# One layer with a product-key expert stage on one core: the first expert rows of the second product, and how the experts in use are found

## The chip, the cores and the metric

One core of a Trainium2 chip runs the whole layer in one launch. Its engines are TensorE (PE: matmuls, with PEld for the weight loads), VectorE (DVE), ScalarE (ACT), GpSimd (POOL) and SyncE (SP); they run side by side and wait for each other by semaphores. The metric is the device time of one launch in microseconds, the median of several runs.

## The reference, cut to what matters

A layer of a diffusion backbone on 256 tokens of 2048 features: a token mixer (projection, two recurrent scans, a spatial gate, output projection), and then the expert stage, at whose middle the change stands. Each token picks 16 of 16384 experts in each of 8 heads by a product of two key tables; each expert has one row u and one row v.

```
idx = e1 * PEER_NKEYS + e2
g = jax.nn.softmax(sc, axis=-1)
u_sel = jnp.take(u_tab, idx, axis=0)
act = jax.nn.gelu(jnp.einsum('td,thkd->thk', hb, u_sel))
v_sel = jnp.take(v_tab, idx, axis=0)
return jnp.einsum('thk,thkd->td', (g * act.astype(jnp.float32)).astype(hb.dtype), v_sel)
```

The result is added to the stream, and a final RMSNorm gives the output.

## The kernel before

The expert stage is computed densely on the one side and by lists on the other. fp32 operands are split in a high and a low part (`split`, lines 255 on ScalarE and 256 on VectorE, half a tile at a time), and a product is the sum of three matmuls of parts (`mm3`, lines 284 to 286).

**The u product.** All 16384 u rows are multiplied with all tokens, in 128 tiles of 128 experts (`u_step`, lines 1188 and 1190). A step's result is evacuated by ScalarE (line 1203), its halves are added on GpSimd (line 1204; on VectorE for the first 8 tiles, lines 1200 and 1201), and in the next step Gelu is applied (`u_out`, line 1209) and the tile is stored to the table `agd` in DRAM (line 1210, ScalarE's queue), which holds for every expert the activations and the gates of all tokens.

**Work beneath it.** `fill` hands out other work between the tiles by credits: 3000 a step, against a cost written beside each piece. In this order: the routing (top 16, softmax), then `gates`, `places`, `make_list`, and the first gathers of v rows. `gates` goes over 32 blocks of 8 tokens: VectorE makes one-hot rows of the two key numbers (line 1025, two a block) and scales one by the gates (line 1034), TensorE multiplies them (`products`): line 1057 gives the gates of all experts, and line 1054 counts, for each half of the tokens (16 blocks), how often an expert was picked. ScalarE keeps the gates (`keep`, line 1067, `GC`), in columns of 4 tokens. From the counts `places` gives every expert in use a place in one of three lists: used by the first token tile only (`N_A` = 26 tiles of 128 rows), by both (up to tile 67), by the second only (up to `N_L` = 92 tiles). `SEQ` is the order in which the tiles of the lists are taken. Experts that find no place are counted in `flag`.

**The seam.** After the last u tile, `act_rows` gathers the activation and gate rows of the first two list tiles from `agd` on GpSimd (line 898, the same line as the v gathers), then every engine loads the flag (line 1290) and branches over a fallback (line 1291) that is run only if an expert found no place. Behind the branch the rows of tiles 2 and 3 are gathered.

**The v product.** `weights` multiplies activations and gates of a list tile (line 1220, VectorE), `weights_high` and `weights_low` split the result (lines 1229 on ScalarE, 1234 on VectorE), and `v_tile` multiplies it with the gathered v rows: 12 matmuls of lines 284 to 286 for a tile of one token tile, 24 for a tile of both. `split_next` prepares the tile after next and gathers rows four tiles ahead.

## Time and profile before

| | us |
|---|---|
| median of 3 runs | 1791.05 |
| lowest, highest | 1789.89, 1794.6 |
| the profiled execution | 1794.17 |
| its span | 1792.4 |
| PE, DVE, ACT, POOL busy in it | 1707.9, 1340.4, 922.0, 401.5 |

The profiled execution is 3.1 us above the median, and its span leaves 1.8 us of its time around it. TensorE is busy in 95% of the span. In the slices of the page it is at nine tenths or more nearly everywhere; the drop at the slices from 1384 us on is the seam. The granted TensorE clock is 0.982 in the mean over the span.

### The profile page before, as it was taken

The numbers are of one execution on the slowest core, as the hardware profiler recorded it, in microseconds if no ns is written. First come the engines' busy times: TensorE is split into PE (matmuls) and PEld (weight loads), VectorE is DVE, ScalarE is ACT, GpSimd is POOL, SyncE is SP. The second block draws the span as 40 slices with busy tenths as digits, with TensorE's granted clock in tenths as the row PEclk, the third lists the DMA queues.
The fourth block names the chain that finished last, engine by engine and source line by source line (L and its number), as shares of the span: only waits on it lengthen the run. The fifth ranks groups of instructions, "written<-read, shape, count | busy, mean of one in ns | idle before, by whom it ended". The sixth has DMA issues, their size and how long they took to land.

```text
span 1792.4 us, 26487 instructions
## 1 busy us (share of the span) xinstructions
PE 1707.9 (95%) x10313; PEld 1422.4 (79%) x10313; DVE 1340.4 (75%) x1812; ACT 922.0 (51%) x1232; POOL 401.5 (22%) x341
## 2 busy tenths in 40 slices
PE   4999999999999999999999999999998799999995
PEld 0778566788799888888888888888887688888884
DVE  1347697687788999898888886988443577777776
ACT  5223666643543455555555555444454465656554
POOL 0000000000100002222222221212112565656652
PEclk8999999999999999999999999999999899999997
DMA  9877778888797656655787888865675789888881
GB/s 394 335 307 281 297 274 323 329 322 299 291 338 283 242 202 215 209 187 184 220 236 227 226 242 235 260 216 189 213 276 189 247 307 350 309 304 307 305 315 59
DMA packets 166266, 472.43 MB, mean 264 GB/s; under 512 B 76692, under 2 KB 109640, under 8 KB 115960
## 3 DMA queue, kind: packets, MB, share of 16 engines
q1 hardware_dynamic: 92544, 316.17, 50.3%
q0 software_dynamic: 21120, 128.68, 20.3%
q10 hardware_dynamic: 52472, 25.84, 5.0%
q8 instruction: 82, 1.34, 0.3%
q14 instruction: 48, 0.39, 0.1%
HBM read 432.81 MB, written 37.83 MB: 263 GB/s over the span
## 4 chain that ended last, share of the span: by engine, by line
PE 80%; DVE 11%; DMA 5%; issue 2%; ACT 2%; POOL 0%; SPq 0%; DVEq 0%; POOLq 0%; ACTq 0%
PE bank L1188 23%; PE bank L284 13%; PE bank L286 12%; PE bank L285 12%; PE bank L1190 12%; DVE ra L256 4%; DMA fa<-in_wm_a_dram 2%; DMA fa<-in_wm_c_dram 2%; PE bank L1057 2%; PE bank L364 1%; PE bank L309 1%; DVE fa L290 1%; DVE fa L942 1%; PE bank L527 1%; DVE fa L940 1%
## 5 line engine op out<-in xcount | busy, mean ns | idle before, releaser
L256 DVE TENSOR_TENSOR ra<-fa,ra 128x1024 fp32r<-128x1024 f32 x564 | 702.0, 1259 | 291.9 <-ACT ra L255 286.2
L255 ACT ACTIVATE ra<-fa 128x1024 fp32r<-128x1024 f32 x564 | 591.3, 1057 | 473.7 <-PE bank L1188 187.3
L1188 PE MATMUL bank<-ra 128*128 128x512 f32 x2048 | 731.9, 401 | 0.0
L1190 PE MATMUL bank<-ra 128*128 128x256 f32 x2048 | 576.9, 282 | 5.1 <-DVE ra L256 5.0
L284 PE MATMUL bank<-ra 128*128 128x512 f32 (+1 forms) x1364 | 475.0, 348 | 17.9 <-ACT ra L1229 16.8
L286 PE MATMUL bank<-ra 128*128 128x512 f32 (+1 forms) x1364 | 468.2, 343 | 5.4 <-DVE ra L1234 4.5
L285 PE MATMUL bank<-ra 128*128 128x512 f32 (+1 forms) x1364 | 467.8, 343 | 1.4 <-DVE ra L256 1.4
L1188 PEld LDWEIGHTS bank<-ra 128*128 128x128 f32 x2048 | 385.8, 188 | 92.6 <-ACT ra L255 0.2
L1190 PEld LDWEIGHTS bank<-ra 128*128 128x128 f32 x2048 | 387.7, 189 | 8.5 <-DVE ra L256 8.4
L284 PEld LDWEIGHTS bank<-ra 128*128 128x128 f32 x1364 | 261.8, 192 | 76.7 <-issue 25.8
L1204 POOL TENSOR_TENSOR fa<-fa 128x256 f32<-128x256 f32 x120 | 150.9, 1258 | 724.2 <-ACT fa L1203 724.1
L286 PEld LDWEIGHTS bank<-ra 128*128 128x128 f32 x1364 | 261.5, 192 | 36.7 <-DVE ra L1234 6.5
L285 PEld LDWEIGHTS bank<-ra 128*128 128x128 f32 x1364 | 261.8, 192 | 32.1 <-DVE ra L256 3.1
L1203 ACT ACTIVATE fa<-bank 128x512 f32<-128x512 f32 x120 | 71.8, 598 | 145.8 <-PE bank L1190 139.8
L898 POOL DMA_INDIRECT fa<-agd,fa x92 | 128.3, 1395 | 39.1 <-issue 26.5
L898 POOL DMA_INDIRECT fa<-in_peer_v_dram,fa x92 | 97.4, 1058 | 119.8 <-DVE ra L256 80.1
L1025 DVE TENSOR_TENSOR fa<-fa 128x1024 f16<-128x1024 bf16 x96 | 113.5, 1223 | 0.0
L1034 DVE TENSOR_TENSOR fa<-fa 128x2048 f16<-128x2048 f16 (+1 forms) x48 | 109.2, 2275 | 0.8
L290 DVE SCALAR_TENSOR_TENSOR fa<-fa 128x2048 f32<-128x2048 f32 x32 | 72.9, 2284 | 0.0
L1209 ACT ACTIVATE fa<-fa 128x256 f32<-128x256 f32 x128 | 52.0, 407 | 33.7 <-DVE fa L1201 25.6
L364 PE MATMUL bank<-fa 128*2 128x512 f32 x256 | 39.6, 711 | 25.5 <-DMA fa<-in_wm_a_dram 17.4
L1229 ACT ACTIVATE ra<-fa 128x128 fp32r<-128x128 f32 x92 | 32.4, 352 | 50.9 <-DVE fa L1220 50.7
(264 smaller groups left out, 1168.1 us busy)
## 6 DMA issues: line engine op xcount, KB each, us to landing
fa<-in_peer_u_dram SPq DMA_DIRECT2D x128, 1024.0 KB, 5.1
fa<-in_wm_a_dram SPq DMA_DIRECT2D x32, 1024.0 KB, 7.8
fa<-in_wm_c_dram SPq DMA_DIRECT2D x32, 1024.0 KB, 6.8
fa<-in_wm_d_dram SPq DMA_DIRECT2D x32, 1024.0 KB, 6.8
fa<-in_w_in_dram SPq DMA_DIRECT2D x24, 1024.0 KB, 4.9
fa<-in_w_out_dram SPq DMA_DIRECT2D x16, 1024.0 KB, 6.7
fa<-in_wq_dram SPq DMA_DIRECT2D x16, 1024.0 KB, 7.4
agd<-fa ACTq DMA_DIRECT2D x128, 128.0 KB, 2.4
```

The lines of the kernel that those rows point to most:

```text
L255: S.activation(h, x, AF.Copy)
L256: V.tensor_tensor(l, x, h.bitcast(F32), op=ALU.subtract)
L284: TE.matmul(dst, wh, mh, start=first, stop=False, skip_group_check=skip)
L285: TE.matmul(dst, wh, ml, start=False, stop=False, skip_group_check=skip)
L286: TE.matmul(dst, wl, mh, start=False, stop=last, skip_group_check=skip)
L290: V.scalar_tensor_tensor(junk, w, 1.0, s, op0=ALU.mult, op1=ALU.mult, accum_out=dst)
L898: G.indirect_dma_start(out=dst, out_offset=None, in_=src, in_offset=bass.IndirectOffsetOnAxis(ap=idx, axis=0), bounds_check=bound, oob_is_ ...
L1025: V.tensor_tensor(dst, iota_b[:, 0:n].unsqueeze(1).to_broadcast([P, TB, n]), numbers.unsqueeze(2).to_broadcast([P, TB, n]), op=ALU.is_equal)
L1034: V.tensor_tensor(og, oj.unsqueeze(2).to_broadcast([P, TB, 2, n]), factors.unsqueeze(3).to_broadcast([P, TB, 2, n]), op=ALU.mult)
L1188: TE.matmul(bank, h[:, es], H2[:, k, :, :].rearrange("p z t -> p (z t)"), start=k == 0, stop=False, skip_group_check=True)
L1190: TE.matmul(bank[:, 0:T], l[:, es], HH[:, k, :], start=False, stop=k == KD - 1, skip_group_check=True)
L1204: G.tensor_tensor(st, HALVES[:, 0:T], HALVES[:, T:2 * T], op=ALU.add)
```

## The change

It has two parts.

Experts in use: the count matmuls of `products` are gone. In `keep`, GpSimd adds up the gates that ScalarE has just stored, over the blocks of a half, in `SUMS` (128 experts by 4 token columns, 512 elements), in two additions a block; at the end of a half VectorE reduces the 4 columns to one (`USED`). `places` takes an expert as in use where this sum is over zero.

Seam: experts of the last three u tiles (from `CUT` = 125) that only the first token tile uses are moved to the list of both, so that the first list needs rows of `agd` from the first 125 tiles alone, and the gather's source is cut to those. `SEQ` begins with four tiles of the first list instead of three. Their rows are gathered in the step of tile 125, and the weights of the first two list tiles are made in the last step (`first_weights`, with a buffer of its own, `WP1`). Tiles 125 to 127 are added on VectorE instead of GpSimd and stored from SyncE's queue. The gathers and weights that stood after the loop and after the branch are gone; the two late v gathers go to `split_next`.

```diff
+CUT = NU - 3
 N_L = N_A + N_1
 ONE_0, BOTH, ONE_1 = list(range(N_A)), list(range(N_A, N_0)), list(range(N_0, N_L))
-SEQ = ONE_0[:3]
+SEQ = ONE_0[:4]
 for _i, _b in enumerate(BOTH):
-    SEQ += [_b] + (ONE_0[3:] + ONE_1)[_i:_i + 1]
+    SEQ += [_b] + (ONE_0[4:] + ONE_1)[_i:_i + 1]
 SEQ += [_s for _s in ONE_1 if _s not in SEQ]
...
     PT = [q_(11520, 128)] + [q_(12288 + 128 * i, 128) for i in range(4)]
+    SUMS = q_(12288, 512).rearrange("p (j t) -> p j t", t=4)
+    USED = [q_(11648 + 128 * i, 128) for i in range(2)]
     STAGE = [q_(12032, 256), q_(14976, 256), dg2]
...
     WP = [dg2, eg[:, 0:256]]
-    HALVES = q_(13824, 512)
+    HALVES, WP1 = q_(13824, 512), q_(11264, 256)
     pidx = small(1)
...
             else:
-                by_index(AGR[n % 4][:, 0:T], ag_half, LIST2[:, j:j + 1], 2 * NE + 1)
+                m = CUT * P + 1 if j < N_A else NE + 1
+                by_index(AGR[n % 4][:, 0:T], ag_half[0:2 * m, :], LIST2[:, j:j + 1], 2 * m - 1)
...
         def products(b):
-            counts = pb[4 + b // NB][:, 0:P]
             oj, og = pair(b, P)
...
                 oa = OHA[b % 2][:, i, :]
-                TE.matmul(counts, oa, oj[:, i, :], start=b % NB == 0 and i == 0,
-                          stop=b % NB == NB - 1 and i == TB - 1, skip_group_check=True)
                 for q in range(2):
...
+            quarter = [GC[c % 2][:, :, o * TB + 4 * x:o * TB + 4 * x + 4] for x in range(2)]
+            if b % NB == 0:
+                G.tensor_tensor(SUMS, quarter[0], quarter[1], op=ALU.add)
+            else:
+                for x in range(2):
+                    G.tensor_tensor(SUMS, SUMS, quarter[x], op=ALU.add)
+            if b % NB == NB - 1:
+                V.tensor_reduce(USED[b // NB], SUMS, axis=AX.X, op=ALU.add)
             if o == HT // TB - 1:
...
         one, tot, inc, pos = PT[0], PT[1], PT[2], PT[3]
-        V.tensor_scalar(u0, pb[4][:, 0:P], 0.5, None, op0=ALU.is_gt)
-        V.tensor_scalar(u1, pb[5][:, 0:P], 0.5, None, op0=ALU.is_gt)
+        V.tensor_scalar(u0, USED[0], 0.0, None, op0=ALU.is_gt)
+        V.tensor_scalar(u1, USED[1], 0.0, None, op0=ALU.is_gt)
         V.tensor_tensor(part[1], u0, u1, op=ALU.mult)
...
         V.tensor_tensor(part[2], u1, part[1], op=ALU.subtract)
+        V.tensor_tensor(part[1][:, CUT:P], part[1][:, CUT:P], part[0][:, CUT:P], op=ALU.add)
+        V.memset(part[0][:, CUT:P], 0.0)
         yield 1500
...
         fill()
+        if n == NU - 1:
+            first_weights()
         u_out(n - 1)
         st = STAGE[n % 3]
-        if n < 8:
+        if n < 8 or n >= CUT:
             S.activation(st, bank[:, T:2 * T], AF.Copy)
...
             S.activation(st, st, AF.Gelu_apprx_tanh)
-            S.dma_start(ag4[n, :, :, 0, :], st.rearrange("p (t i) -> p t i", t=2))
+            (nc.sync if n >= CUT else S).dma_start(ag4[n, :, :, 0, :], st.rearrange("p (t i) -> p t i", t=2))
...
             ag = AGR[n % 4][:, 0:u * T].rearrange("p (t z i) -> p t z i", t=u, z=2)
-            V.tensor_tensor(WP[n % 2][:, span_of(n)].rearrange("p (t i) -> p t i", t=u), ag[:, :, 0, :],
-                            ag[:, :, 1, :], op=ALU.mult)
+            V.tensor_tensor(wp(n).rearrange("p (t i) -> p t i", t=u), ag[:, :, 0, :], ag[:, :, 1, :], op=ALU.mult)
+    def wp(n):
+        return (WP1 if n == 1 else WP[n % 2])[:, span_of(n)]
+    def first_weights():
+        for n in range(2):
+            weights(n)
+            weights_high(n)
+            weights_low(n)
...
         if n < N_L:
-            S.activation(WS[n % 3][0][:, span_of(n)], WP[n % 2][:, span_of(n)], AF.Copy)
+            S.activation(WS[n % 3][0][:, span_of(n)], wp(n), AF.Copy)
...
             c = span_of(n)
-            V.tensor_tensor(WS[n % 3][1][:, c], WP[n % 2][:, c], WS[n % 3][0][:, c].bitcast(F32), op=ALU.subtract)
+            V.tensor_tensor(WS[n % 3][1][:, c], wp(n), WS[n % 3][0][:, c].bitcast(F32), op=ALU.subtract)
...
         u_step(n, fill)
+        if n == CUT:
+            for i in range(4):
+                act_rows(i)
         if n in (1, 2):
...
-    for n in range(2):
-        act_rows(n)
-    gather(late.pop(0))
...
             act_rows(n + 4)
+            if late:
+                gather(late.pop(0))
             weights(n + 2)
...
-    for n in range(2, 4):
-        act_rows(n)
-    gather(late.pop(0))
-    for n in range(2):
-        weights(n)
-        weights_high(n)
-        weights_low(n)
     norm0 = None
...
```

How the instructions stand now is shown at three places. GpSimd beneath the u product, before, from the table of list places to the first gather of v rows (L1204 adds the halves of a u tile):

```order
L1013 IOTA fa 128x1
L1204 TENSOR_TENSOR fa<-fa 128x256 x57
L1124 DMA ptab<-fa 128x128
L1204 TENSOR_TENSOR fa<-fa 128x256 x28
L898 DMA fa<-in_peer_v_dram,fa 128x2048
```

The same place in the change (L1220 is the former L1204; L1075 and L1078 are the sums):

```order
L1019 IOTA fa 128x1
L1220 TENSOR_TENSOR fa<-fa 128x256 x4
L1075 TENSOR_TENSOR fa<-fb 128x512
L1220 TENSOR_TENSOR fa<-fa 128x256 x2
L1078 TENSOR_TENSOR fa<-fa,fb 128x512 x2
L1220 TENSOR_TENSOR fa<-fa 128x256
```

Between every one or two additions of u halves stand two sums, each over twice the elements.

GpSimd at the seam, before (gathers of v rows and of `agd`, then the load of the flag and the branch):

```order
L898 DMA fa<-in_peer_v_dram,fa 128x2048
L1204 TENSOR_TENSOR fa<-fa 128x256
L898 DMA fa<-agd,fa 128x256 x2
L898 DMA fa<-in_peer_v_dram,fa 128x2048
L1290 TENSOR_LOAD fa
L1291 COMPARE_AND_BRANCH
```

The same place in the change (L903 is the former L898):

```order
L1220 TENSOR_TENSOR fa<-fa 128x256
L903 DMA fa<-in_peer_v_dram,fa 128x2048
L1220 TENSOR_TENSOR fa<-fa 128x256 x2
L903 DMA fa<-agd,fa 128x256 x4
L903 DMA fa<-in_peer_v_dram,fa 128x2048 x2
L1313 TENSOR_LOAD fa
L1314 COMPARE_AND_BRANCH
```

All four row gathers now stand ahead of the branch and of two v gathers, and no addition of a u tile follows them.

VectorE at the seam, before (the splits, then the flag):

```order
L1156 CAST fa<-fa 128x92
L256 TENSOR_TENSOR ra<-fa,ra 128x1024 x44
L1286 TENSOR_REDUCE fa<-fa 128x1
L1288 CAST fa<-fa 128x1
L1290 TENSOR_LOAD fa
L1291 COMPARE_AND_BRANCH
```

The same place in the change (L259 are the splits, L1217 the additions of u tiles, L1236 and L1258 the weights and their low parts):

```order
L259 TENSOR_TENSOR ra<-fa,ra 128x1024 x2
L1236 TENSOR_TENSOR fa<-fa 128x128
L1258 TENSOR_TENSOR ra<-fa,ra 128x128
L1236 TENSOR_TENSOR fa<-fa 128x128
L1258 TENSOR_TENSOR ra<-fa,ra 128x128
L1217 TENSOR_TENSOR fa<-bank_77,fa 128x256
L1309 TENSOR_REDUCE fa<-fa 128x1
L1311 CAST fa<-fa 128x1
L1313 TENSOR_LOAD fa
L1314 COMPARE_AND_BRANCH
```

The weights of two tiles and the addition of the last u tile now stand between the last split and the flag.

## Rows read from the trace of the kernel before

**Rows 1.** The page, part 1: busy us (share of the span) xinstructions.

```profile
PE 1707.9 (95%) x10313; PEld 1422.4 (79%) x10313; DVE 1340.4 (75%) x1812; ACT 922.0 (51%) x1232; POOL 401.5 (22%) x341
```

**Rows 2.** Windows: us; PE, PEld, DVE, ACT, POOL busy; PEclk, DMA share, GB/s; second: L1034.

```profile
827.84:1029.12 201.28, 201.28 (x1461) 176.11 (x1460) 176.14 (x121) 108.10 (x163) 47.70 (x31) 1.00 0.77 222
...
827.84:1029.12 201.28, 47.40 (x20) 1.00 0.77 222
```

**Rows 3.** PE's waits 580 to 640: us, times, longest; then a timeline row.

```profile
PE bank L1190 <- DVE ra L256: 3.7, 6, 0.9
...
900.43 1.06 ACT L255 ACTIVATE ra<-fa 128x1024 fp32r<-128x1024 f32 x1 [1.17 <-PE bank L1188]
```

**Rows 4.** Timeline at the seam: start, us, engine, line; the wait before, its releaser.

```profile
1371.08 0.52 ACTq L1210 DMA_DIRECT2D agd<-fa  x1
...
1382.08 1.23 DVE L256 TENSOR_TENSOR ra<-fa,ra 128x1024 fp32r<-128x1024 f32 x1 [0.99 <-ACT ra L255]
...
1383.41 0.15 DVE L1288 CAST fa<-fa 128x1 uint32<-128x1 f32 x1
...
1383.61 0.28 PE L1190 MATMUL bank<-ra 128*128 128x256 f32 x1
...
1385.82 0.52 ACTq L1210 DMA_DIRECT2D agd<-fa  x1
1391.02 1.02 POOL L898 DMA_INDIRECT fa<-agd,fa  x1 [5.68 <-DMA agd<-fa]
...
1393.85 0.29 DVE L1220 TENSOR_TENSOR fa<-fa 128x128 f32<-128x128 f32 x1 [10.29 <-DMA fa<-agd,fa]
...
1394.52 0.29 DVE L1234 TENSOR_TENSOR ra<-fa,ra 128x128 fp32r<-128x128 f32 x1 [0.38 <-ACT ra L1229]
1394.54 0.80 PE L284 MATMUL bank<-ra 128*128 128x512 f32 x1 [10.65 <-ACT ra L1229]
```

**Rows 5.** After the seam: windows (PEclk third from last), then timeline of PE.

```profile
1394.50:1399.00 4.50, 4.46 (x11) 3.49 (x12) 0.88 (x3) 1.26 (x2) 0.15 (x1) 0.50 0.68 239
1399.00:1402.40 3.40, 3.38 (x15) 2.44 (x13) 0.00 (x0) 0.00 (x0) 1.16 (x2) 1.00 0.00 0
...
1404.53 0.50 PE L284 MATMUL bank<-ra 128*128 128x512 f32 x1 [2.15 <-ACT ra L1229]
...
1412.65 0.41 PE L284 MATMUL bank<-ra 128*128 128x512 f32 x1
```

**Rows 6.** Timeline of PE in one block's burst, first and last triples.

```profile
903.36 0.22 PE L1054 MATMUL bank<-fa 128*128 128x128 f16 x1
...
904.37 0.22 PE L1054 MATMUL bank<-fa 128*128 128x128 f16 x1
```

**Rows 7.** Timeline of GpSimd and VectorE in the gates; the last row after them.

```profile
897.01 2.36 DVE L1025 TENSOR_TENSOR fa<-fa 128x1024 f16<-128x1024 bf16 x2
...
898.39 1.57 POOL L1204 TENSOR_TENSOR fa<-fa 128x256 f32<-128x256 f32 x1 [5.57 <-ACT fa L1203]
899.30 1.75 DVE L256 TENSOR_TENSOR ra<-fa,ra 128x1024 fp32r<-128x1024 f32 x1
...
904.87 2.90 DVE L1025 TENSOR_TENSOR fa<-fa 128x1024 f16<-128x1024 bf16 x2
...
1094.79 0.73 POOL L1204 TENSOR_TENSOR fa<-fa 128x256 f32<-128x256 f32 x1 [5.56 <-ACT fa L1203]
```

**Rows 8.** Timeline, a GpSimd addition of 128x512 near the end.

```profile
1757.48 1.28 POOL L1371 TENSOR_TENSOR fb<-fb,fa 128x512 f32<-128x512 f32 x1 [3.19 <-DVE fb L1368]
```

**Rows 9.** Groups by line, shapes apart: xcount, busy us, mean ns, idle before.

```profile
L1209 ACT ACTIVATE fa<-fa 128x256 f32<-128x256 f32 x128 | 52.0, 407 | 33.7 <-DVE fa L1201 25.6 <-DVE fa L1019 5.4 <-POOL fa L1204 2.6
...
L1201 DVE TENSOR_TENSOR fa<-bank,fa 128x256 f32<-128x256 f32 x8 | 3.3, 417 | 0.0
L1200 ACT ACTIVATE fa<-bank 128x256 f32<-128x256 f32 x8 | 3.1, 385 | 4.5 <-ACT fa L1209 3.2 <-PE bank L1190 1.3
```

**Rows 10.** The flag's branch by engine: ns min/median/max, first and last start.

```profile
L1291 PEldq COMPARE_BRANCH  x1: 3366/3366/3366, 1384.2 to 1384.2; - x1
```

## The prediction

> **What bounds the kernel now.** I read the page first: TensorE is busy for 95% of the span [rows 1], so a microsecond is won only where TensorE has less to do or waits less. Then the table by stretches, for the two places that the change touches.
>
> The first is the stretch in which the gate rows are made, 32 blocks of 8 tokens beneath the u product. In it 20 blocks, counted by their 20 wide products of line 1034, take 201.28 us, 10.06 us a block. TensorE is busy for all of it, VectorE for 176.14 us, 8.81 us a block [rows 2]. So TensorE is the bound and VectorE has 1.25 us to spare per block. GpSimd is at 24%.
>
> The second is the seam between the u product and the v product. TensorE's last u matmul starts at 1383.61, the first v matmul at 1394.54 after 10.65 us of waiting for the first tile's weights [rows 4]. The granted clock then is 0.50, the lower of its two levels, 1.2 GHz, and TensorE stops again before it comes back for good [rows 5].
>
> **The counts leave TensorE.** The 256 matmuls of line 1054, one a token, go. In a burst, seven triples of one count matmul and two of line 1057 start 0.168 us apart (903.36 to 904.37, six intervals), so a matmul costs 0.056 us [rows 6]. Per block that is 8 x 0.056 = 0.45 us, in all 256 x 0.056 = 14.3 us, all of it on the engine that sets the end. TensorE would then need 10.06 - 0.45 = 9.61 us a block.
>
> **The sums on GpSimd are not free.** What replaces them is 62 additions of 128x512 on GpSimd, two a block (one in the first block of each half). GpSimd has the time; the question is what they do to VectorE. The trace shows it on GpSimd's additions of line 1204, 128x256. Alone one takes 0.73 us. Beside VectorE it takes twice that: it starts inside a VectorE instruction, ends some 0.6 us after that one, and the next VectorE instruction is longer by about as much: a split of line 256 takes 1.75 us instead of 1.23, a pair of line 1025 2.90 instead of 2.36 [rows 7]. All 50 of this stretch take at least 1.09 us, most 1.50 to 1.80, as the first of these rows. So the two engines take turns, and a 256-element addition takes 0.53 us from VectorE. A 128x512 addition alone takes 1.28 us [rows 8], 0.55 more than the 0.73 for 256 elements; that slope, 2.1 ns an element, also gives the 0.53 for 256, so a new addition should take 512 x 2.1 ns = 1.08 us from VectorE. The ends: 0.53, if the turn doesn't grow with the size, and 1.28, if it lasts the whole instruction. I take 1.08, since both rows lie on its slope.
>
> VectorE then needs 8.81 + 2 x 1.08 = 10.97 us a block where TensorE needs 9.61. The order of work by credits is unchanged, so nothing is postponed, and over 32 blocks VectorE falls behind by 32 x 1.36 = 43 us. Some of that is absorbed: the split of a tile's second half waits for TensorE to be half through the tile two before it [rows 3], so it is about 10 us early, but the routing stage ahead has used part of this up (TensorE already waits there for splits [rows 3]). I take 6 us, between 0 and 10; it is caught up later, where VectorE has room. TensorE then waits 43 - 6 = 37 us and saves 14.3: **about 23 us lost** here. At 0.53 a sum it is 9.87 against 9.61, 8 us over 32 blocks, nearly all absorbed: 2 - 14 = 12 us won. At 1.28 it is 11.37 a block, 56 us, 50 after absorption: 36 us lost.
>
> One rule of the Trainium skill would make it worse. Its page SBUF — State Buffer, section "SBUF: two separate sides", says that VectorE instructions with two SBUF inputs and GpSimd share a port pair as an exclusive lock, held for the whole instruction. By that rule a sum costs VectorE 1.28 us and the time is the second rival's, 1816. The rows show the exclusion, but 0.53 us lost for an instruction of 0.73, so I keep the slope. The same page, section "Specifications (TRN2)", gives SBUF lines of 16 bytes that want two hits each for full speed; the sums read the gates in runs of 4 fp32, four hits, so by it the stride costs nothing. No row here shows a strided addition on GpSimd.
>
> Small things of this part: two VectorE reductions of 128x512 to 128, each waiting for the last sum, at most 0.6 us of work plus one pair of sums already counted; VectorE only waits there if it is not late. ScalarE's Gelu of the tile before waits for GpSimd's addition of line 1204, now queued behind up to two sums. Three turns take 6 to 8 us and a step about 7, so ScalarE may wait a microsecond; it is 54% busy there and its splits are ahead of VectorE, so I count nothing. If that cover fails, it adds to the loss.
>
> **The seam.** The rows of the first four tiles now come from the first 125 u tiles. They are gathered on GpSimd at the 126th, after the store of tile 124, and nothing is queued behind them on GpSimd but v gathers, since tiles 125 to 127 are combined on VectorE. Until now the first gather started 5.2 us after the issue of the last store (1385.82 to 1391.02), and its rows were there 2.8 us later. Counted from the store of tile 124, issued at 1371.08 [rows 4], the second gather starts by 1377.6 and is landed at 1380.4, before the last splits are through; I count no wait. The first two tiles' weights follow VectorE's last split, which ends at 1383.31. A tile takes 0.96 us there (product, high part, low part: 1393.85 to 1394.81) [rows 4], so 1385.2. ScalarE's Gelu of tile 126, 0.41 us, follows the second high part: 1384.9 to 1385.3. Then the copy of the last bank, 0.385 us, and VectorE's addition, 0.417 us [rows 9]: 1386.1. The two instructions on the flag ended 0.25 us after the split before them, at 1383.56 [rows 4]: 1386.35.
>
> Here stands a wait that stays. Every engine loads the flag and branches over the fallback. On TensorE the branch ran from 1384.2 for 3.37 us, to 1387.6 [rows 10]: 4.0 us after the flag. Until now the late rows hid this; now it is the last wait, and it comes later, since the flag follows the last tile's addition on VectorE. TensorE would start at 1386.35 + 4.0 = 1390.4 instead of 1394.54.
>
> More is won after it. By 1412.65, when the clock is back for good, 39 v matmuls had started [rows 5]. At full clock they start 0.23 us apart (15 in 3.40 us) [rows 5], 9.0 us; from 1383.85 that is 28.8 - 9.0 = 19.8 us lost at the seam. Part of this was the second pair of gathers, which stood behind the branch and cost a second wait and a second slow stretch. In the change they are in before it. Left are 6.5 us of waiting and one slow stretch like the first, some 11 matmuls in 4.5 us where 2.5 would do [rows 5]: 2.0 us. That is 8.5, so **11 us won**. Next late is VectorE, with 3.1 us for a one-user tile (two splits of 1.23, product and low part of 0.29) against TensorE's 12 x 0.23 = 2.8: from 1390.4 it has tile 2 at 1393.6, tile 3 at 1396.7, before TensorE wants them. Bounds: 4 us if the fifth tile's rows, gathered only after the branch, bring the second stop back (it and its slow stretch cost 7 us: 15 matmuls from 1402 to 1412.65); 13 us if the clock doesn't fall.
>
> **Sum.** The profiled execution took 1794.17 us, 3.1 more than the median 1791.05. 1794.2 + 23 - 11 = 1806, against the median 1803.
>
> **Rivals.** First, VectorE keeps up: the turns cost it 0.53 us a sum, or fall into its 1.25 us of idleness. Then the counts' 14 us are won, but for 2, with the seam's 11: 1791 - 12 - 11 = 1768. For it: the 0.53 is measured, 1.08 is a slope. Against it: idleness of 1.25 us a block shrinks to 0.80 when TensorE gets quicker, and the sums need 2.16. Up to 0.89 us a sum the whole change is no slower than before: (2 x 0.89 - 0.80) x 32 = 31 us of lag, just the 6 absorbed, the counts' 14 and the seam's 11.
>
> Second, the turn lasts the whole instruction, or the strided read makes it longer: 1791 + 36 - 11 = 1816; at 2 us a sum 12.81 a block, 102 us of lag, 1791 + 82 - 11 = 1862. For it: no row shows a strided addition on GpSimd. Against it: 0.53 of 0.73 us is what a whole instruction takes now. The lock rule of the Trainium skill's page SBUF — State Buffer, named above, would give the 1816.
>
> Third, the seam gives only 4 us, with the gates as forecast: 1810. Fourth, the change doesn't do what it says, since moving early experts to the shared list overflows it and the fallback runs, over 256 gathers of 1.0 us [rows 4] at the least: beyond 2050. On the reference's inputs the list ends at 8532 of 8576, so hardly.
>
> **How the numbers follow.** Forecast 0.50, 1792 to 1814 on its own (0.93 to 1.23 us a sum); VectorE keeps up 0.22, 1764 to 1772; a cost between these two 0.05; whole turns or slower 0.16, half of it over 1820; small seam 0.06; fallback 0.01. Cases of both signs hold most of the chance, so the range reaches from 1766 to 1820 and leaves out about 0.15. About 0.3%, 5.4 us, is what can be told from no change. Faster by more: 0.22 and most of the 0.05, 0.26. Within: the low end of the forecast, 0.11. Slower: 0.63.
>
> **What would show it.** In the profile of the changed kernel: blocks 10.9 us apart instead of 10.06, VectorE busy for nearly all of that stretch, TensorE waiting for splits (L256, now 259), GpSimd's sums at 2 us or more with VectorE's next instruction about 1.1 us longer. If the blocks come 9.6 us apart and TensorE doesn't wait, the first rival holds. At the seam: one wait of about 6.5 us that ends with TensorE's branch, one stretch at 0.50 clock, and no second stop. I am wrong if VectorE's instructions aren't longer beside the sums, if the sums take longer than 1.3 us alone, or if TensorE waits at the seam for rows.

## The result: 1806.5 us, and the profile after

The changed kernel took 1806.51 us (median of four runs, 1805.25 to 1809.67) beside 1792.01 for the kernel before (four runs): a ratio of 1.0097, 95% interval 1.0067 to 1.0126. It is slower by 14.5 us, with a forecast of 1803. The profiled execution took 1806.62 us, its span is 1804.5 us.

Lines have moved by a few numbers: the splits L255/L256 are L258/L259 now, the u product L1188/L1190 is L1202/L1204, the gate products L1057 are L1060, the wide products L1034 are L1040, GpSimd's addition L1204 is L1220, the v product L284 to L286 is L287 to L289, the v weights L1220/L1229/L1234 are L1236/L1253/L1258, and the branch L1291 is L1314. New are the sums, L1075 and L1078.

The page's first part answers to [rows 1], with busy us, share of the span and instructions:

```profile
PE 1697.1 (94%) x10057; PEld 1412.6 (78%) x10057; DVE 1403.5 (78%) x1819; ACT 922.1 (51%) x1232; POOL 547.3 (30%) x400
```

TensorE has the 256 count matmuls fewer and is busy 10.8 us less; GpSimd is busy 146 us more, as meant. What was not asked for is VectorE's line: only seven instructions more, but 63 us more work.

Cut at three places that every run has (the first and the last of the 32 wide products of the gates, the end of the last u matmul), the two spans show where the time went:

| us | first to last wide product | first wide product to end of u | wait before v | end of u to end of span |
|---|---|---|---|---|
| before | 316.2 | 613.8 | 10.65 | 408.5 |
| after | 342.1 | 637.1 | 8.42 | 399.4 |
| difference | +25.9 | +23.3 | -2.2 | -9.1 |

So both halves of the forecast are there, a loss beneath the u product and a gain at the seam, +23.3 - 9.1 = +14.2 us. The first wide product itself comes 2.1 us earlier after than before (768.01 and 770.12); no edit stands ahead of it.

**The gates.** The table by stretches from the first to the last wide product, of before and then of after (us; busy PE, PEld, DVE, ACT, POOL with instructions; PEclk, DMA share, GB/s), on the same ends as each other, a longer cut than [rows 2]:

```profile
770.12:1086.35 316.23, 316.23 (x2272) 276.51 (x2271) 279.39 (x193) 171.20 (x256) 78.39 (x49) 1.00 0.75 220
```

```profile
768.01:1110.15 342.14, 317.06 (x2082) 275.92 (x2081) 338.68 (x193) 176.19 (x262) 214.36 (x109) 0.97 0.70 205
```

Before, the first number after the length repeats the length: TensorE never stops. After, it is VectorE that is busy for 338.68 of 342.14 us, with 193 instructions, as many as before. The bound has changed hands. Blocks come 342.14 / 31 = 11.04 us apart.

VectorE's instructions are longer because GpSimd's sums run beside them. The timeline, first of GpSimd and then of VectorE (start, us, then engine, line and operation; in brackets the idle time before it):

```profile
904.66 4.35 POOL L1078 TENSOR_TENSOR fa<-fa 128x512 f32<-128x512 f32 x2 [2.37 <-ACT fa L1070]
...
911.18 5.01 POOL L1078 TENSOR_TENSOR fa<-fa 128x512 f32<-128x512 f32 x2 [0.49 <-ACT fa L1070]
```

```profile
899.42 2.28 DVE L1040 TENSOR_TENSOR fa<-fa 128x2048 f16<-128x2048 f16 x1
...
904.43 3.43 DVE L1031 TENSOR_TENSOR fa<-fa 128x1024 f16<-128x1024 bf16 x2
...
911.70 3.36 DVE L1040 TENSOR_TENSOR fa<-fa 128x2048 f16<-128x2048 f16 x1
```

The wide product takes 2.28 us with no sum beside it and 3.36 beside one, 1.08 more. The pair of one-hots takes 3.43 beside a sum, where it took 2.36 alone [rows 7]. These sums take over 2 us each, where a 128x512 addition alone took 1.28 [rows 8].

TensorE then waits, but not where I had looked. Its waits from 768 to 1125 (us in total, times, longest):

```profile
PE bank L1060 <- DVE fa L1040: 24.9, 8, 5.5
PE bank L1060 <- ACT fb L1070: 3.0, 1, 3.0
```

It waits for the wide products, in a few lumps, not for splits. One lump, and the table by stretches of the 3.9 us behind it and of the 8 us after that:

```profile
838.14 1.89 PE L1060 MATMUL bank<-fa 128*128 128x128 f16 x16 [5.51 <-DVE fa L1040]
```

```profile
838.10:842.00 3.90, 3.86 (x25) 3.59 (x26) 3.90 (x4) 0.00 (x0) 0.56 (x1) 0.61 0.19 78
842.00:850.00 8.00, 8.00 (x48) 7.06 (x47) 8.00 (x8) 4.01 (x6) 3.08 (x1) 1.00 0.62 192
```

After 5.51 us without work the granted clock (third number from the end) is 0.61 over the next 3.9 us, so most of them at the lower level of 1.2 GHz, and 1.00 after that.

**The seam.** Gathers, VectorE, the branch and TensorE, in four cuts of the timeline and of the branch's line (ns min/median/max, first and last start):

```profile
1395.19 1.02 POOL L903 DMA_INDIRECT fa<-agd,fa  x1 [5.62 <-DMA agd<-fa]
```

```profile
1404.41 0.28 DVE L1236 TENSOR_TENSOR fa<-fa 128x128 f32<-128x128 f32 x1
...
1407.10 0.15 DVE L1311 CAST fa<-fa 128x1 uint32<-128x1 f32 x1
```

```profile
L1314 PEldq COMPARE_BRANCH  x1: 4946/4946/4946, 1408.2 to 1408.2; - x1
...
L1314 DVEq EVENT_SEMAPHORE  x1: 21/21/21, 1412.4 to 1412.4; - x1
```

```profile
1413.50 0.77 PE L287 MATMUL bank<-ra 128*128 128x512 f32 x1 [8.42 <-PEq L1314]
```

The gathers of the rows start ten microseconds before the u product ends at 1405.08, the first weights follow the last split at once, and the wait that is left ends with TensorE's branch, at 1413.2. VectorE's first event behind its own branch is 0.8 us earlier, at 1412.4. The second stop and second slow stretch of [rows 5] are gone: from 1380 to 1440 the view of waits has one more entry, 0.7 us.

### The profile page after: what moved, and what is told of

It reads as the page before. It is cut to its first block, busy times and chain, and to the rows that moved or that the text cites. A ratio compares the mean times of both kernels' runs of the same rounds, so it can differ in the third digit from the quotient of the medians.

```text
span 1804.5 us, 26114 instructions
## 1 busy us (share of the span) xinstructions
PE 1697.1 (94%) x10057; PEld 1412.6 (78%) x10057; DVE 1403.5 (78%) x1819; ACT 922.1 (51%) x1232; POOL 547.3 (30%) x400
## 5 line engine op out<-in xcount | busy, mean ns | idle before, releaser
L259 DVE TENSOR_TENSOR ra<-fa,ra 128x1024 fp32r<-128x1024 f32 x564 | 725.2, 1305 | 243.4 <-ACT ra L258 235.3
L258 ACT ACTIVATE ra<-fa 128x1024 fp32r<-128x1024 f32 x564 | 591.1, 1057 | 485.6 <-PE bank L1202 198.8
L1202 PE MATMUL bank<-ra 128*128 128x512 f32 x2048 | 734.2, 402 | 0.0
L1204 PE MATMUL bank<-ra 128*128 128x256 f32 x2048 | 577.6, 282 | 5.3 <-DVE ra L259 5.2
L287 PE MATMUL bank<-ra 128*128 128x512 f32 (+1 forms) x1364 | 473.7, 347 | 13.9 <-PEq L1314 8.4
L289 PE MATMUL bank<-ra 128*128 128x512 f32 (+1 forms) x1364 | 466.7, 342 | 3.9 <-DVE ra L1258 3.0
L1202 PEld LDWEIGHTS bank<-ra 128*128 128x128 f32 x2048 | 389.1, 190 | 91.5 <-ACT ra L258 0.3
L1204 PEld LDWEIGHTS bank<-ra 128*128 128x128 f32 x2048 | 390.6, 191 | 8.9 <-DVE ra L259 8.9
L1220 POOL TENSOR_TENSOR fa<-fa 128x256 f32<-128x256 f32 x117 | 161.6, 1381 | 540.8 <-ACT fa L1219 540.8
L287 PEld LDWEIGHTS bank<-ra 128*128 128x128 f32 x1364 | 260.7, 191 | 72.3 <-issue 25.1
L289 PEld LDWEIGHTS bank<-ra 128*128 128x128 f32 x1364 | 260.3, 191 | 34.9 <-DVE ra L1258 4.5
L903 POOL DMA_INDIRECT fa<-agd,fa x92 | 132.3, 1438 | 41.7 <-issue 26.2
L1031 DVE TENSOR_TENSOR fa<-fa 128x1024 f16<-128x1024 bf16 x96 | 141.1, 1509 | 0.0
L903 POOL DMA_INDIRECT fa<-in_peer_v_dram,fa x92 | 99.3, 1079 | 109.5 <-DVE ra L259 65.2
L1040 DVE TENSOR_TENSOR fa<-fa 128x2048 f16<-128x2048 f16 (+1 forms) x48 | 119.5, 2489 | 0.8
L1078 POOL TENSOR_TENSOR fa<-fa 128x512 f32<-128x512 f32 x32 | 72.0, 2251 | 26.6 <-ACT fa L1070 25.3
L367 PE MATMUL bank<-fa 128*2 128x512 f32 x256 | 39.7, 713 | 25.9 <-DMA fa<-in_wm_a_dram 17.8
```

The lines of the kernel that those rows point to most:

```text
L258: S.activation(h, x, AF.Copy)
L259: V.tensor_tensor(l, x, h.bitcast(F32), op=ALU.subtract)
L287: TE.matmul(dst, wh, mh, start=first, stop=False, skip_group_check=skip)
L289: TE.matmul(dst, wl, mh, start=False, stop=last, skip_group_check=skip)
L903: G.indirect_dma_start(out=dst, out_offset=None, in_=src, in_offset=bass.IndirectOffsetOnAxis(ap=idx, axis=0), bounds_check=bound, oob_is_ ...
L1031: V.tensor_tensor(dst, iota_b[:, 0:n].unsqueeze(1).to_broadcast([P, TB, n]), numbers.unsqueeze(2).to_broadcast([P, TB, n]), op=ALU.is_equal)
```

## Experiments

All ratios are to the kernel before, run on the same chip beside each group of runs; three chips were used (medians of before 1791.2, 1787.0 and 1787.5 us), so ratios are compared, not times. The chips also differ in the stretch of the gates. The early flag's run below, on the second chip, has the same work in it as the kernel before, all count products and no sums, and takes 311.38 us at a granted clock of 1.00 where the kernel before took 316.23; the run with seven tiles, on the third, takes 311.37. Why is open. So stretches are compared on chips that agree on this.

```profile
763.47:1074.85 311.38, 311.38 (x2273) 274.04 (x2272) 279.33 (x193) 171.12 (x256) 72.88 (x49) 1.00 0.76 224
```

**The two parts by themselves.** First the seam alone: the changed kernel with the sums out and the count products back.

```diff
+                TE.matmul(counts, oa, oj[:, i, :], start=b % NB == 0 and i == 0,
+                          stop=b % NB == NB - 1 and i == TB - 1, skip_group_check=True)
...
-                    G.tensor_tensor(SUMS, SUMS, quarter[x], op=ALU.add)
...
-        V.tensor_scalar(u0, USED[0], 0.0, None, op0=ALU.is_gt)
+        V.tensor_scalar(u0, pb[4][:, 0:P], 0.5, None, op0=ALU.is_gt)
```

> The changed seam alone; the 256 count products stay on TensorE and GpSimd has no sums. Theory (the sums lose, the seam gains): the gates take 316 us from the first to the last scaled product as before, the u product ends within 1 us of before, the seam gains 9, so about 1783 us (1779 to 1787). Rival (the new seam costs as well, or gains only because the u product ran late and everything else was ready): 1788 to 1796.

Measured: 1780.46 us, ratio 0.9945 (0.9920 to 0.9971), 10.7 us faster on the medians, and 401.6 us from the end of u to the end of the span instead of 408.5. The gates are as before. The table by stretches from the first to the last wide product, then the restart:

```profile
766.27:1082.52 316.25, 316.25 (x2272) 276.44 (x2271) 279.36 (x193) 171.09 (x256) 78.37 (x49) 1.00 0.75 220
```

```profile
1389.19 0.76 PE L287 MATMUL bank<-ra 128*128 128x512 f32 x1 [8.56 <-DVE fa L1231]
```

The seam is a gain of its own and doesn't need a late u product. Its wait is as long as in the changed kernel.

Then the sums alone, put into the kernel before in place of its count products, with the seam untouched:

```diff
-                TE.matmul(counts, oa, oj[:, i, :], start=b % NB == 0 and i == 0,
-                          stop=b % NB == NB - 1 and i == TB - 1, skip_group_check=True)
...
+                for x in range(2):
+                    G.tensor_tensor(SUMS, SUMS, quarter[x], op=ALU.add)
```

> The sums on GpSimd alone, count products gone, the seam as before. Theory: the u product ends 21 us later as in the changed kernel and the seam gives nothing back: about 1813 us (1809 to 1818), VectorE 11.0 us a block of 8 tokens. Rival (the lag came from the new seam's transfers and order): at most 1797.

Measured: 1811.01 us, ratio 1.0135 (1.0098 to 1.0172). The stretch of the gates is 341.99 us, the changed kernel's to 0.2 us, and the way from the first wide product to the end of u 636.0 us. The parts multiply to 0.9945 x 1.0135 = 1.0079, within the interval of the whole change.

**Which engine sets the pace.** Both counts at once: the changed kernel with the 256 count products put back on TensorE, their result unread.

```diff
...
+                TE.matmul(counts, oa, oj[:, i, :], start=b % NB == 0 and i == 0,
+                          stop=b % NB == NB - 1 and i == TB - 1, skip_group_check=True)
...
```

> The changed kernel with the 256 count products put back on TensorE, their result not read. Theory (VectorE sets the pace of the gates at 11.04 us a block, TensorE waits 27.8 us there): the 14.3 us of products fill waiting time, 1806 to 1812 us, and the waits of TensorE for the scaled one-hots fall from 18 us towards 8. Rival (TensorE sets the pace, the sums cost nothing by themselves): 1819 to 1823 us.

Measured: 1804.79 us, ratio 1.0078 (1.0041 to 1.0114). That is no slower than without them; the time lies 1.2 us under the expected range. Stretch and waits (the latter in that same stretch, and then in the changed kernel's own):

```profile
768.47:1110.56 342.09, 328.17 (x2329) 287.44 (x2328) 341.77 (x194) 175.31 (x262) 202.78 (x109) 0.98 0.70 205
```

```profile
PE bank L1063 <- DVE fa L1040: 13.9, 6, 3.1
```

```profile
PE bank L1060 <- DVE fa L1040: 22.0, 7, 5.5
```

TensorE got its 13 us of matmuls back, they went into its waiting, and the stretch has not moved by 0.1 us. VectorE, busy for 341.77 of 342.09 us, sets the pace.

Neither count: the sums out and nothing in their place, so that the list is empty and the second product runs on weights of zero.

```diff
-                    G.tensor_tensor(SUMS, SUMS, quarter[x], op=ALU.add)
...
+                V.memset(USED[b // NB], 0.0)
```

> The changed kernel without the sums on GpSimd and without the count products: nothing counts the use of experts, so the list is empty and the second product runs on weights of zero. Theory (TensorE would set the pace again at 9.6 us a block): the u product ends 14 us earlier than with the new seam alone, about 1769 us (1765 to 1774). Rival (VectorE or ScalarE holds the gates anyway once the products are gone): 1776 to 1783 us.

Measured: 1769.69 us, ratio 0.9892 (0.9857 to 0.9926).

```profile
764.97:1067.82 302.85, 302.85 (x2032) 263.02 (x2031) 278.62 (x193) 171.22 (x256) 77.57 (x49) 1.00 0.78 230
```

TensorE is busy throughout again, and the count products were worth 316.25 - 302.85 = 13.4 us of this stretch, which holds 240 of the 256.

This run is also the yardstick for the changed kernel. Their stretches of the gates don't hold the same matmuls (2082 and 2032), but from the first wide product to the end of the u product both have 3801 (changed kernel first):

```profile
768.01:1405.08 637.07, 608.27 (x3801) 527.80 (x3799) 542.77 (x395) 319.44 (x460) 282.14 (x172) 0.98 0.70 214
```

```profile
764.97:1364.40 599.43, 598.71 (x3801) 519.24 (x3799) 480.26 (x395) 318.45 (x460) 138.96 (x110) 1.00 0.75 227
```

The changed kernel takes 37.6 us longer. TensorE idles 28.8 us instead of 0.7, and is busy 9.6 us longer with the same matmuls, at a mean granted clock of 0.98 instead of 1.00. Since VectorE sets the pace, the lower clock costs nothing on top; it fills the wait.

**How the price of a sum scales.** Half the width: the 62 sums over the first 64 of each 128 experts, the others left out and taken as unused.

```diff
-            quarter = [GC[c % 2][:, :, o * TB + 4 * x:o * TB + 4 * x + 4] for x in range(2)]
+            quarter = [GC[c % 2][:, 0:64, o * TB + 4 * x:o * TB + 4 * x + 4] for x in range(2)]
...
```

> The changed kernel with sums of half the width: 62 GpSimd sums of 128x256, over the first 64 experts of each group of 128 (the use of the others is left out and counts as none). Theory (each sum takes VectorE's time in proportion to its elements, near 1 us at 128x512, so near 0.5 here): VectorE works 10.0 us a block, the scaled products span 310 to 318 us instead of 342, about 1778 us (1772 to 1786). Rival (the price goes by the number of sums, or by their order behind the kept gates): near the changed kernel, 1798 to 1807.

Half the number: 32 instructions of 128x512, over four of every eight tokens.

```diff
...
-                for x in range(2):
-                    G.tensor_tensor(SUMS, SUMS, quarter[x], op=ALU.add)
+                G.tensor_tensor(SUMS, SUMS, quarter, op=ALU.add)
```

> The changed kernel with half the sums: 32 GpSimd instructions of 128x512, over the first four of every eight tokens (the others are left out of the counting). Theory (time by elements): as with sums of half the width, 310 to 318 us from the first to the last scaled product, about 1778 us (1772 to 1786). Rival (VectorE is held only when two sums stand in a row, or the first of a pair sets the price): under 1772 or over 1790.

Measured: 1772.91 us, ratio 0.9914 (0.9887 to 0.9941), and 1769.13 us, ratio 0.9898 (0.9854 to 0.9943). The stretches, half the width first:

```profile
768.07:1078.24 310.17, 305.62 (x2076) 266.01 (x2075) 309.82 (x195) 174.38 (x260) 170.60 (x108) 1.00 0.77 225
```

```profile
764.28:1074.15 309.87, 304.10 (x2058) 264.86 (x2057) 309.21 (x194) 173.14 (x258) 135.73 (x80) 0.99 0.77 225
```

Against the 279.4 us that VectorE works without sums (279.33 on the second chip, on which the halves ran), the full sums cost it 338.68 - 279.4 = 59.3 us. Of the 62 sums 59 lie in this stretch, so one costs 1.00 us. At half the width 58 sums cost 30.4 us, 0.52 each; at half the number 30 cost 29.8 us, 0.99 each. (0.6 to 0.7 us of each difference is VectorE's own work at the end of a half.) The price goes by the elements, about 2.0 ns each in all three, and not by the number of instructions. The time of the second lies 3 us below its expected range; the chip's kernel before was 4 us faster too.

**What the seam's wait consists of.** The two VectorE instructions on the flag were moved up to the place where the flags are made; count products stay on TensorE.

```diff
         V.tensor_scalar(flag[:, 2:3], flag[:, 2:3], float(N_L * P), None, op0=ALU.is_gt)
+        V.tensor_reduce(flag[:, 0:1], flag, axis=AX.X, op=ALU.add)
+        V.tensor_copy(pidx.bitcast(U32), flag[:, 0:1])
...
-    V.tensor_reduce(flag[:, 0:1], flag, axis=AX.X, op=ALU.add)
...
-    V.tensor_copy(flagu, flag[:, 0:1])
```

> The new seam with count products on TensorE, and the two VectorE instructions that reduce the flag and turn it into an integer moved up to where the flags are made, some 200 us before the seam. Theory (the wait at the seam is the flag, then the load of the flag and the branch): the wait of 8.56 us falls by the 2.0 us between the last u product and the flag, to about 6.5, and the time by the same, about 1778 us. Rival (the branch is fetched while the flag is on its way, or VectorE's own restart decides): the wait stays over 8 us and the time at 1780.

Measured: 1780.92 us, ratio 0.9953 (0.9932 to 0.9973), not to be told from the seam alone. The profiled execution is the fastest of its ten, 10.7 us under their median; its first wide product comes at 763.5 us, 8.5 before that of the next run's profile, so most of that lead lies ahead of the cuts used here. The wait falls to 7.2 us, not 6.5. TensorE's and VectorE's branches, then the restart:

```profile
L1309 PEldq COMPARE_BRANCH  x1: 3366/3366/3366, 1369.3 to 1369.3; - x1
...
L1309 DVEq COMPARE_BRANCH  x1: 63/63/63, 1374.2 to 1374.2; - x1
...
L1309 DVEq EVENT_SEMAPHORE  x1: 21/21/21, 1379.0 to 1379.0; - x1
```

```profile
1379.19 0.77 PE L287 MATMUL bank<-ra 128*128 128x512 f32 x1 [7.18 <-DVEq L1309]
```

TensorE is through its branch at 1372.7, but starts only when VectorE is through its own. VectorE reaches the branch after its last addition, at 1374.2, and its next event is 4.8 us later. So the wait is VectorE's restart, the second half of the rival, though the wait is under the 8 us that the rival named. The expectation was wrong in taking TensorE's branch as the last to end.

Next the fallback was left out altogether, with flag, load and branch:

```diff
-    more = nc.values_load(flagu[0:1, 0:1], min_val=0, max_val=3)
-    with tc.If(more > 0):
...
```

> The new seam with count products on TensorE, and without the fallback: no flag, no load of it, no branch (the part for lists that are too long, which this input does not enter, is left out). Theory (the branch is what TensorE waits for): the v product begins within 2 us of the last u product, which gives 6.5 to 9 us, and as many again as the clock doesn't fall, up to 5: 1767 to 1774 us. Rival (the weights of the first v tiles are the next wait, or the clock falls anyway): 1775 to 1780.

Measured: 1783.0 us, ratio 0.9979 (0.9961 to 0.9997). The v product starts 0.07 us after the u product, as expected, but the time is not the 1767 to 1774 us expected, and nothing is won: 400.1 us from the end of u to the end of the span, where the early flag had 396.5. The timeline of GpSimd and of TensorE:

```profile
1380.17 1.00 POOL L903 DMA_INDIRECT fa<-in_peer_v_dram,fa  x1 [1.83 <-DVE fa L1231]
1389.95 1.00 POOL L903 DMA_INDIRECT fa<-agd,fa  x1 [8.79 <-DVE ra L1253]
```

```profile
1394.27 0.50 PE L287 MATMUL bank<-ra 128*128 128x512 f32 x1 [2.20 <-ACT ra L1248]
1396.81 0.80 PE L289 MATMUL bank<-ra 128*128 128x512 f32 x1 [1.41 <-DVE ra L1253]
```

The gather at 1389.95 is the fifth tile's, the first that needs rows of the last u tile. The row names VectorE, but in the code this gather also depends on the stores of the last u tiles. The two last stores issue between 1381.71 and 1383.40, and the view of DMA issues from 1360 to 1420 has a median of 6.3 us from issue to landing for them and one earlier store, which comes to about 1389. TensorE has four one-sided tiles to fill the time, some 11 us, and then stops in steps.

To see whether it is that store, the same kernel got seven early tiles at the front in place of four:

```diff
-SEQ = ONE_0[:4]
+SEQ = ONE_0[:7]
...
```

> The new seam without flag, load and branch, as in the run before (the fallback is left out), and with seven v tiles on early rows at the front in place of four. Theory (without the branch, the fifth tile's gather waits for the store of the last u tile, which sets TensorE's next stop): with three more early tiles, 12 products each, that stop goes and the v part is 5 to 9 us shorter than the 400.1 us without the branch, ratio to before 0.990 to 0.994. Rival (the early tiles' one-sided rows make the gathers and splits the bound there): v part 398 us or longer, ratio 0.997 as with four.

Measured: 1770.68 us, ratio 0.9907 (0.9887 to 0.9927), and 390.1 us after the end of u, 10 less than with four tiles. Gather and clock (GpSimd's timeline; then the table from 1384 to 1400, first with four tiles, then with seven, PEclk third from the end):

```profile
1379.67 1.11 POOL L903 DMA_INDIRECT fa<-agd,fa  x1 [0.30 <-issue]
```

```profile
1384.00:1400.00 16.00, 12.27 (x45) 8.85 (x44) 8.31 (x11) 6.44 (x9) 8.10 (x7) 0.85 0.63 221
```

```profile
1384.00:1400.00 16.00, 13.29 (x53) 9.16 (x51) 11.87 (x18) 8.96 (x13) 9.50 (x9) 1.00 1.03 409
```

The fifth gather no longer waits, and the clock stays up. So behind the branch's wait stood that for the last store, nearly as long, and taking the branch away paid only when that went too. Seven early tiles with the branch in place were not run.

**A version that beats both.** The new seam with the early flag, and the use of experts counted without GpSimd: the first 32 of every 128 tokens by products on TensorE, the other 96 by three VectorE reductions of the kept gates, 128x4096 each.

```diff
+                if b % NB < 4:
+                    TE.matmul(pb[4 + b // NB][:, 0:P], oa, oj[:, i, :], start=b % NB == 0 and i == 0,
...
+            if b % NB > 6 and b % 4 == 3:
+                V.tensor_reduce(SUMS[:, :, b // 4 % 4], GC[c % 2][:, :, o * TB - 24:o * TB + 8], axis=AX.X, op=ALU.add)
...
```

> The new seam with the early flag, and the use of experts counted without GpSimd: of every 128 tokens the first 32 by count products on TensorE, the other 96 by three VectorE reductions of 128x4096 over the kept gates. Theory (VectorE itself pays about 1.1 ns an element, by the 1.28 us less the share of waiting; the 128x512 reduction took 0.68 us, which bounds one of 128x4096 at 4.3 to 5.4; GpSimd's sums cost it 1.9 ns an element): VectorE 9.0 + 0.8 to 1.1 us a block, TensorE 9.8 + 0.1, so the scaled products span 306 to 312 us and the time falls by 5 to 10 us under the new seam alone, ratio to before 0.987 to 0.992. Rival (the lumps of 4.3 us stop TensorE as the pairs of sums did, and its clock falls): ratio 0.995 or more.

Measured: 1771.61 us, ratio 0.9915 (0.9897 to 0.9933), the fastest of the kernels that compute all. Four of the six reductions (busy us, mean ns) and the stretch of the gates:

```profile
L1079 DVE TENSOR_REDUCE fa<-fa 128x128 f32<-128x4096 f32 x4 | 17.6, 4412 | 0.0
```

```profile
767.47:1075.20 307.73, 305.85 (x2126) 267.69 (x2125) 297.16 (x201) 172.92 (x258) 78.69 (x50) 1.00 0.77 225
```

A gate costs VectorE 4.41 us / 4096 = 1.08 ns when it adds it up itself, and about 2.0 ns when GpSimd does. TensorE is busy for 305.85 of 307.73 us. The expected range of 306 to 312 us doesn't tell much, though, since on this chip the stretch takes 311.4 us with all count products. The way from the first wide product to the end of the u product, of this kernel and then of the run with seven tiles, which ran on the same chip and has all count products:

```profile
767.47:1372.01 604.54, 599.73 (x3864) 522.16 (x3862) 503.72 (x405) 318.50 (x460) 137.04 (x110) 1.00 0.74 225
```

```profile
770.15:1378.69 608.54, 607.64 (x4057) 530.96 (x4055) 481.01 (x393) 318.45 (x460) 134.35 (x110) 1.00 0.74 224
```

193 matmuls fewer, at 0.056 us [rows 6], would be 10.8 us; 4.0 are won, since TensorE now idles 4.8 us and not 0.9, and is busy 2.9 us longer than that sum gives. The ratio's interval meets that of the early flag alone (0.9932 to 0.9973) only at its edge, and overlaps that of the seam alone (0.9920 to 0.9971): faster than the kernel before and than the changed one is shown, faster than the seam alone is likely.

## Why the prediction was right, point by point

**The bound changes hands: right.** VectorE was to need 10.97 us a block and works 338.68 / 31 = 10.93, with blocks 11.04 us apart. That hits closer than its terms. The work without sums was taken as 8.81 from a cut of 201 us [rows 2]; over the whole stretch it is 279.39 / 31 = 9.01. The sums were taken as 2 x 1.08 = 2.16 a block and cost 59.3 / 31 = 1.91, 1.00 each. That the two errors nearly cancel is luck.

**The slope: right.** The runs with half the width and half the number show the price in proportion to elements. The 1.08 us stand in the rows where a sum runs beside a VectorE instruction; 1.00 is the mean over all. The lock rule of the Trainium skill's page SBUF — State Buffer, section "SBUF: two separate sides", held for whole instructions, would make a sum of 1.28 us cost 1.28; the trace agrees that the two engines hold each other up, and not on the size, and the measured 1.00 decides.

**Which engine waits: right, where: wrong.** I had TensorE waiting for splits. It waited 24.9 us for the wide products, in eight lumps of up to 5.5. The step that failed read the waits of an earlier stage [rows 3], where splits are the late instruction; in the gates they are not the ones that end last. The lumps brought what the sum didn't have, a lower clock. The prediction's 37 us of waiting are the 37.6 us by which the changed kernel's u product ends later than that with neither count: 28.1 us more waiting and 9.6 us more busy time. The terms of the 37 hit less well than their difference. The lag was to be 43 us, of which 6 are absorbed. Over the stretch of the gates it is 342.14 - 302.85 = 39.3 us, since TensorE needs 302.85 / 31 = 9.77 us a block without counts and not 9.61, and 1.7 of it are gone at the end of the u product. The 6 were a guess between 0 and 10, and here too errors cancel. ScalarE's wait for GpSimd, counted at nothing, was 9.8 us in six waits; TensorE waited for ScalarE once, for 3.0 us.

**The counts' 14.3 us: right on size, without effect.** They measured 13.4 us between the seam alone and neither count for the 240 in the stretch, 14.3 for all 256 at that rate. In the changed kernel they bought nothing, as putting them back showed. The loss at the end of u was to be 23 and is 23.3.

**The seam: right in kind, 11 us forecast and 9.1 found.** One wait, one slow stretch, no second stop, the wait ended by TensorE's branch. The wait was 8.4 us, not 6.5: the mis-sized term is the 4.0 us from flag to start, which took 6.25 (1407.25 to 1413.50), with a branch of 4.95 us instead of the 3.37 of [rows 10]. The sum also had no term for VectorE's restart, which comes at 1412.4, 5.2 us after the flag. With the early flag it is what TensorE waits for, so a branch of 3.37 us would hardly have brought the 4.0 here. That the branch can take either is shown (3.37 again with the early flag, 5.02 with the seam alone, 6.65 with neither count); why is open. It was a measured duration of one execution, and I gave it no range. The slow stretch was as forecast: ten matmuls 0.43 us apart. The 9.1 is the difference of two single executions: in those of the seam alone and of the changed kernel with both counts the way from the end of u to the end of the span is 401.6 and 402.4 us, 6 to 7 us under the 408.5.

**The rivals.** VectorE keeps up (1768) fell: its break-even of 0.89 us a sum lies under the 1.00. Half the sums came near its time (ratio 0.9898, where 1768 would be 0.987). Whole turns (1816) fell on size. So did a price on the strided read: the sums cost about 2.0 ns an element, the rows without stride gave 2.1. The small seam gain (1810) fell on the missing second stop, and the fallback did not run.

## What to carry to other kernels

Work moved to an idle engine is not free if its instructions there lengthen those of a neighbour that has little slack: read from the trace what an instruction there adds to its neighbour, per element, and hold the sum against the bound's slack per block, not against the idle share of the engine that takes it on. A sum that the busy engine does itself can be cheaper than the same sum beside it. And before paying for the removal of a wait, look for the transfer that runs beneath it; here the wait for the last store stood behind that for the branch.

## What was not expected of the hardware

- A GpSimd sum with two inputs in SBUF cost VectorE about 2.0 ns an element, more than the 1.08 ns an element of VectorE's own reduction of the same gates.
- The same branch over the fallback took TensorE between 3.37 and 6.65 us in different kernels (4.95 in the changed one), and VectorE went on 3.8 us (changed kernel) and 4.8 us (early flag) after reaching it, though its branch is listed with 0.06 us. The Trainium skill's page Runtime: NRT & Kernel Launch, section "Instruction fetch mechanics", says that a taken branch to a far target has to fetch the target's instructions before it goes on. It gives no time for this, and no run here moved the target, so that this is the cause is not shown.
- The granted clock fell behind TensorE's lumps of idle time inside an otherwise dense stretch (0.61 over the 3.9 us behind the one of 5.51 us), and from the first wide product to the end of the u product the changed kernel's TensorE was busy for 608.3 us with matmuls that took 598.7 us where the granted clock was 1.00 throughout.
